# Layer A's out-projection as seven products for eight, in a two-layer f32 trunk

## The chip, the cores and the metric

The kernel runs on one core of one Trainium2 chip. The metric is the device time of one execution in microseconds; of several runs the median counts.

## The reference

Two layers x <- x + mixer(RMSNorm(x)), then a last RMSNorm; x is 2048 x 1024, f32. Both layers end in an out-projection of a 2048 x 1536 tensor z onto 1024 columns:

```python
# layer A
u = h @ w_in                      # 1024 -> 3072: gate, xb
xb = causal_depthwise_conv(xb, conv_w, conv_b)
y = rg_lru(xb, gate_w, gate_b, lam)
x = x + (y * silu(gate)) @ w_out  # z = y * silu(gate)
# layer B
u = h @ w_in                      # 1024 -> 6144: bg, cg, xv, gate
y = bg * causal_depthwise_conv(cg * xv, conv_w)
x = x + (y * silu(gate)) @ w_out
```

## The kernel before, in words

Everything lies transposed: channels on the 128 partitions (P), tokens in four chunks of CH = 512 columns, two chunks to a half. WIDTH = 1536 is twelve blocks of 128 (NH = 12, six pairs KH), 1024 output channels are eight row blocks (KB).

An f32 product is made from f16 parts. Each operand is scaled and split into a high part (ACT, L1119) and a low part (DVE, L1120); `mm3` (L497) issues three matmuls of 128x128 by 128x512, high by high (L500), high by low (L503), low by high (L504). The scale of z comes from its squares: `z_square` (L764) sums the squares of each block on ACT (L769), `scale_from` (L776) sums these over the partitions by a small matmul pt (L780) and works out the scale on DVE (L783 to L789, L1113).

Layer A's in-projection (`in_A`, from about L808) goes through six pairs of heads, for each first the convolution and gates, then SiLU gate and z (L863); the recurrence is a scan on DVE (L906), ahead of it a product on POOL (L905) that uses ACT's square root (L902). Each z is stored to DRAM by `store_z` (L757). Its out-projection is the class `OutProj` (L1126): chunk by chunk, row block by row block, plain block products, 4 x 8 x 12 x 3 matmuls. For chunk 0 the first ten blocks (EARLY) go ahead with a scale of their own (zse), so that their loads and splits run while the in-projection still goes on.

Layer B's two projections use seven products for eight (the form of Strassen and Winograd): a product of 2x2 blocks becomes seven products of sums of blocks. `SEVEN` gives for each name the operand (B11, B21, B22 are blocks of z, T1 to T4 differences), and which output it goes to; A11, A12, A22 and S1 to S4 are blocks and sums of the weights. For layer B's out-projection, `OutSums` (L1304) runs the names in `ORDERS` over each half of the tokens, four row blocks each. `fetch` is its list of loads in order of due time in steps of one row block (a z load at 9 - 2k/3 steps ahead of its product), `splits` that of its splits (6 - 2k/3 ahead). The sums of weights were made in B's in-projection (`weights`) and stored.

Each engine works through its instructions in one order, which the program's scheduler fixes; loads follow one another on SP's queue as `in_order` (L1079) chains them. `defer` and `tick` (L643, L646) put an operation off by some steps, `advance` (L656) gives side work one step beside each group of products. Beside the out-projection `emitA` (L1587) adds the residual, stores x for layer B and adds up its squares on POOL (L230), `besideA` prepares the first operands hB of layer B's in-projection (norms L305, splits L311 and L313).

Of the kernel before, what the change touches and what calls it, by code (L numbers as in the profile page):

```python
# [14 lines left out]
P = 128  # L15
# [31 lines left out]
def trunk(ctx, tc, xT, xn, prm, wa, ga, oa, wb, ob, out):  # L47
# [11 lines left out]
    zd = {  # L59
        (k, c): dr.tile([2 * P, CH], F32, name=f"z{k}_{c}", tag=f"z{k}_{c}")  # L60
        for k in range(NH // 2)
        for c in range(4)
    }

    zt = {
        (half, n, k): dr.tile([P, CH], F32, name=f"z{n}{half}_{k}", tag=f"z{n}{half}_{k}")
# [5 lines left out]
        (n, k): dr.tile([P, 2, CH], F16, name=f"w{n}_{k}", tag=f"w{n}_{k}")  # L72
        for n in ("A11", "A12", "A22", "S1", "S2", "S3", "S4")
# [582 lines left out]
    def advance(side):  # L656

        tick()
        if extra:
            extra[0][0] += 1  # L660
            if extra[0][0] % 3 == 0 and next(extra[0][1], "end") == "end":
                extra.pop()
        while side and next(side[0], "end") == "end":
            side.pop(0)
# [93 lines left out]
    def store_z(kp, m, half, c, z):  # L758
        rows = slice(m * P, (m + 1) * P)
        stores.append(sp.dma_start(zd[kp, 2 * half + c][rows, :], z))  # L760
# [48 lines left out]
    def in_A(ops, first, head, side, before_end, beside):  # L809
# [6 lines left out]
        def pair(hp):  # L816
            heads = (2 * hp, 2 * hp + 1)
            us, tails, sg, gw, taps, gu = {}, {}, {}, {}, [], []

            def conv(m, half, c, a, undo=None):  # L820
# [3 lines left out]
                us[m, half, c] = u = buf(wk, "u", "u", 12)  # L824
# [93 lines left out]
            def xafter(half):  # L918
                side.extend([mixer(half, 0), mixer(half, 1)])
                if half and hp == NH // 2 - 1:  # L920
                    before_end(None)

            def silu(m, half, c, a, undo):
# [7 lines left out]
                sg[m, half, c] = t = buf(wk, "sz", "sg", 8)  # L931
# [8 lines left out]
            def gafter(half):  # L940
                if half == 0 and hp == NH // 2 - 1:
                    before_end(marks[-1])

            units.append((wa[2 * hp], xdest, nothing, beside, xafter, conv))
            units.append((wa[2 * hp + 1], nothing, nothing, beside, gafter, silu))
# [6 lines left out]
    def in_B(ops, first, side, before_end, beside):  # L952
        units = []

        def pair(jp):
# [64 lines left out]
            def gdone(m, half, c, t):  # L1020
# [3 lines left out]
                if late(half):  # L1024
                    g.tensor_tensor(out=t, in0=y, in1=th, op=ALU.mult)
                    z_done(m, half, c, t)
# [3 lines left out]
            def bdone(m, half, c, t):  # L1030
# [3 lines left out]
                else:  # L1034
                    g.tensor_tensor(out=t, in0=t, in1=y, op=ALU.mult)
                    z_done(m, half, c, t)

            zs = {}

            def z_done(m, half, c, z):  # L1040

                zs[m, half, c] = z

                def keep_z(name, t):
                    stores.append(sp.dma_start(zt[half, name, jp], t))

                def diff(name, out, x, y):
                    g.tensor_tensor(out=out, in0=x, in1=y, op=ALU.subtract)
                    keep_z(name, out)

                t1, t2, t4 = cg[0, half, 0], cg[0, half, 1], cg[1, half, 1]
                if (m, c) != (0, 1):
                    keep_z(f"B{m + 1}{c + 1}", z)
                z_square(z, jp, m, half, c, 2 if jp == NH // 2 - 1 or (m, c) == (0, 1) else SQUARED)
                if (m, c) == (0, 1):
                    diff("T1", t1, z, zs[0, half, 0])
                if (m, c) == (1, 1):
                    diff("T2", t2, z, t1)
                if (m, c) == (1, 0):
                    diff("T3", zs[0, half, 1], zs[1, half, 1], zs[0, half, 1])  # L1060
                    diff("T4", t4, z, t2)
# [30 lines left out]
    zse = keep(3)  # L1092

# [3 lines left out]
    LAST = NH // 2 - 1  # L1097
    EARLY = 2 * LAST

# [26 lines left out]
    class OutProj:  # L1126

        def __init__(self, wdram, wsc):  # L1130
            self.wdram, self.wsc = wdram, wsc
            self.rawz, self.raww, self.zops, self.wops = {}, {}, {}, {}
            self.plan, self.done = self.operands(), 0

        def load_z(self, c, kp):
            for m in range(2):
                t = buf(wp, "zr", "zr", 10)
                in_order(sp.dma_start(t, zd[kp, c][m * P : (m + 1) * P, :]))
                self.rawz[2 * kp + m, c] = t

        def load_w(self, k, dh):
            t = buf(wp, "wo", "wo", 8)
            n = (2 * k + dh) * CH
            in_order(sp.dma_start(t, self.wdram[:, n : n + CH]))
            self.raww[k, dh] = t

        def z(self, k, c, zs):
            self.zops[k, c] = split_out(opp, "zs", 22, self.rawz.pop((k, c)), zs[:, 0:1])

        def w(self, k, dh):  # L1150
            if (k, dh) not in self.raww:
                self.load_w(k, dh)
            raw = self.raww.pop((k, dh))
            self.wops[k, dh] = split_out(wp, "wf", 5 * KH, raw, self.wsc[:, 0:1])

        def operands(self):

            for k in range(EARLY):
                self.w(k, 0)
                self.z(k, 0, zse)  # L1160
                yield
            for k in range(EARLY):
                self.w(k, 1)
                yield
            for k in range(EARLY, NH):
                for dh in range(2):
                    self.w(k, dh)
                    yield
            for c in range(4):
                out_scales(zsq[c], zsc[c], self.wsc)  # L1170
                for k in range(0 if c else EARLY, NH):
                    self.z(k, c, zsc[c])
                    yield

        def upto(self, n):
            while self.done < n:
                next(self.plan, None)
                self.done += 1

        def early(self):  # L1180
            out_scales(zsq[0][:, 0:EARLY], zse, self.wsc)

        def start(self, anchor):

            loads.append(anchor)
            for kp in range(LAST):
                self.load_z(0, kp)
                for m in range(2):
                    if kp < 3:
                        self.load_w(2 * kp + m, 0)  # L1190

        def ahead(self):
            for k in range(EARLY):
                self.upto(k + 1)
                yield

        def run(self, emit, end_chunk, side, rest, kept):
            late, xrs = [], {}
            order, fetched = [(c, d) for c in range(4) for d in range(KB)], [0]

            def lag(n):
                while len(late) > n:
                    late.pop(0)()

            def residuals(n):
                while fetched[0] < min(n + XAHEAD, len(order)):
                    c, d = order[fetched[0]]
# [95 lines left out]
    }  # L1303

    class OutSums:

# [551 lines left out]
```

## Time and profile before

| | |
|---|---|
| runs | 1982.82, 1981.59, 1982.82 us; median 1982.82 |
| the profiled execution | 1984.61 us, of which the span from first to last instruction is 1982.7 |
| granted TensorE clock, mean | 0.996 of full speed |
| busy of the span | PE 1959.7 us, DVE 1194.6, ACT 1063.5, POOL 597.6 |
| out-projection of A | its matmuls start at 617.6 and end at 870.4 us; 249.72 us busy |
| data moved | 216.25 MB, mean 109 GB/s |

PE is TensorE, PEld its weight loads, DVE VectorE, ACT ScalarE, POOL GpSimd, SP the engine whose queue starts most transfers. Matmuls overlap: the busy time of a single one is longer than the step from one start to the next. A row of waits names the waiting instruction and the one that released it.

### The profile page before, as it was taken

How to read it: one execution, taken by the hardware profiler on the slowest of the kernel's cores; microseconds unless marked ns; L12 is line 12 of the kernel's file. 1: busy time of each engine (PE TensorE's matmuls, PEld its weight loads, DVE VectorE, ACT ScalarE, POOL GpSimd, SP SyncE). 2: the span in 40 equal slices, each digit the busy share in tenths (PEclk: the TensorE clock that was granted, in tenths of full speed). 3: DMA queues.
4: the chain of work that ended last, by engine and by line, in shares of the span. 5: the costliest groups of instructions: out<-in, count | busy, mean ns of one | idle time of the engine just before them, and what ended most of it. 6: DMA issues, size and time to landing. Idle time of an engine off the chain costs nothing.

```text
span 1982.7 us, 25189 instructions
## 1 busy us (share of the span) xinstructions
PE 1959.7 (99%) x9064; PEld 915.8 (46%) x9064; DVE 1194.6 (60%) x2041; ACT 1063.5 (54%) x1912; POOL 597.6 (30%) x486
## 2 busy tenths in 40 slices
PE   8999999999999999999999999999999999999998
PEld 4444444444444444444444444444444444444446
DVE  7977665667675755379535656746626336454565
ACT  7878786868585533155644443544453452454442
POOL 0001000101000311143553673664553443522221
PEclk9999999999999999999999999999999999999999
DMA  8111212151304734421241241242130030397462
GB/s 299 64 54 59 91 54 88 46 171 44 110 11 138 232 108 160 92 95 43 86 144 43 80 165 43 91 149 70 64 112 32 22 107 22 132 381 258 119 200 86
DMA packets 130958, 216.25 MB, mean 109 GB/s; under 512 B 13200, under 2 KB 41488, under 8 KB 130832
## 3 DMA queue, kind: packets, MB, share of 16 engines
q1 hardware_dynamic: 130384, 213.58, 32.8%
q8 instruction: 71, 1.16, 0.3%
q0 software_dynamic: 448, 1.06, 0.2%
q14 instruction: 55, 0.45, 0.1%
HBM read 152.19 MB, written 62.40 MB: 108 GB/s over the span
## 4 chain that ended last, share of the span: by engine, by line
PE 90%; DVE 6%; ACT 2%; DMA 1%; issue 1%; POOL 0%; SPq 0%; DVEq 0%; ACTq 0%
PE acc L504 15%; PE acc L503 15%; PE acc L500 15%; PE p L504 8%; PE p L500 8%; PE p L503 8%; PE r L500 4%; PE r L504 4%; PE r L503 4%; PE pg L880 3%; PE q L504 2%; PE q L500 2%; PE q L503 2%; DVE op L313 1%; DVE u L843 1%
## 5 line engine op out<-in xcount | busy, mean ns | idle before, releaser
L500 PEld LDWEIGHTS <-wc 128*128 128x128 f16 x2096 | 207.9, 99 | 255.0 <-issue 18.2
L504 PEld LDWEIGHTS <-wc 128*128 128x128 f16 x2096 | 205.2, 98 | 257.4 <-issue 14.2
L503 PEld LDWEIGHTS <-wc 128*128 128x128 f16 x2096 | 205.1, 98 | 257.2 <-issue 22.6
L500 PE MATMUL p<-op,wc 128*128 128x512 f16 x768 | 290.7, 379 | 2.3 <-ACT wc L420 1.2
L503 PE MATMUL p<-op,wc 128*128 128x512 f16 x768 | 291.1, 379 | 0.0
L504 PE MATMUL p<-op,wc 128*128 128x512 f16 x768 | 290.6, 379 | 0.4 <-DVE wc L421 0.4
L503 PE MATMUL acc<-op,wc 128*128 128x512 f16 x752 | 285.4, 380 | 2.8 <-DVE op L313 2.8
L504 PE MATMUL acc<-op,wc 128*128 128x512 f16 x752 | 285.7, 380 | 0.0
L500 PE MATMUL acc<-op,wc 128*128 128x512 f16 x752 | 283.3, 380 | 1.3 <-ACT op L311 1.3
L905 POOL TENSOR_TENSOR u<-fixed,u 128x512 f32<-128x512 f32 x48 | 51.3, 1090 | 557.8 <-ACT fixed L902 557.8
L421 DVE SCALAR_TENSOR_TENSOR wc<-ws,fixed,wc 128x512 f16<-128x512 f32 x104 | 103.4, 999 | 84.7 <-ACT wc L420 74.6
L421 DVE SCALAR_TENSOR_TENSOR wc<-wr,fixed,wc 128x512 f16<-128x512 f32 x122 | 106.9, 894 | 78.0 <-ACT wc L420 66.1
L500 PE MATMUL acc<-zs,wf 128*128 128x512 f16 x384 | 145.5, 379 | 0.0
L503 PE MATMUL acc<-zs,wf 128*128 128x512 f16 x384 | 145.5, 379 | 0.0
L504 PE MATMUL r<-op,wc 128*128 128x512 f16 x384 | 145.5, 379 | 0.0
L503 PE MATMUL r<-op,wc 128*128 128x512 f16 x384 | 145.5, 379 | 0.0
L500 PE MATMUL r<-op,wc 128*128 128x512 f16 x384 | 145.5, 379 | 0.0
L504 PE MATMUL acc<-zs,wf 128*128 128x512 f16 x384 | 145.2, 379 | 0.0
L504 PE MATMUL acc<-op,wf 128*128 128x512 f16 (+1 forms) x384 | 135.3, 352 | 0.0
L503 PE MATMUL acc<-op,wf 128*128 128x512 f16 (+1 forms) x384 | 135.3, 352 | 0.0
L500 PE MATMUL acc<-op,wf 128*128 128x512 f16 (+1 forms) x384 | 135.3, 352 | 0.0
L230 POOL TENSOR_TENSOR sa<-sa,sq 128x512 f32<-128x512 f32 x48 | 67.1, 1398 | 224.9 <-ACT sq L229 177.7
(200 smaller groups left out, 3410.6 us busy)
## 6 DMA issues: line engine op xcount, KB each, us to landing
wr<-in_wb SPq DMA_DIRECT2D x104, 256.0 KB, 3.5
xs<-in_xT SPq DMA_DIRECT2D x48, 256.0 KB, 6.0
z<-sg SPq DMA_DIRECT2D x48, 256.0 KB, 2.0
zr<-z SPq DMA_DIRECT2D x48, 256.0 KB, 5.2
zr<-zT SPq DMA_DIRECT2D x48, 256.0 KB, 5.4
wr<-in_wa SPq DMA_DIRECT2D x44, 256.0 KB, 4.1
zB<-ed SPq DMA_DIRECT2D x36, 256.0 KB, 2.0
zT<-cg SPq DMA_DIRECT2D x36, 256.0 KB, 2.0
```

The source lines that it names most:

```text
L230: squared[0] = eng.tensor_tensor(out=acc, in0=acc, in1=sq, op=ALU.add)
L313: return hi, v.tensor_tensor(out=t[:, 1, :], in0=src, in1=t[:, 0, :], op=ALU.subtract)
L421: v.scalar_tensor_tensor(out=t[:, 1, :], in0=src, scalar=sw[:, 2:3], in1=t[:, 0, :], op0=ALU.mult, op1=ALU.subtract,)
L500: ins = nc.tensor.matmul(acc, wh, xh, start=start, stop=False, **kw)
L503: nc.tensor.matmul(acc, wh, xl, start=False, stop=False, **kw)
L504: return nc.tensor.matmul(acc, wl, xh, start=False, stop=stop, **kw)
L843: v.scalar_tensor_tensor(out=u[:, n:], in0=a[:, 0 : CH - n], scalar=ac(3 - n), in1=u[:, n:], op0=ALU.mult, op1=ALU.add,)
L880: ins = nc.tensor.matmul(pg, gw[m][:, oo], u, start=True, stop=True)
L905: g.tensor_tensor(out=u, in0=w, in1=u, op=ALU.mult)
```

## The change

- `OutProj` goes; layer A's out-projection is an `OutSums("A", ...)`: half 0 in the order S1, S4, A12, A11, S2, S3, A22, half 1 in A11, S2, S3, A22, A12, S1, S4; 2 x 7 x 4 x 6 x 3 matmuls. (Layer B's is the same class; the halved last chunks are for B alone.)
- z's differences T1 to T4 are made on POOL in A's in-projection and stored with the blocks (`z_done`, now shared by both layers).
- The sums S1 and S4 of the weights are made and split in A's in-projection, and stored (12 pairs); the other five names (STAY) are made beside half 0 from raw weights (`load_raw`, `make_w`), and stay for half 1.
- One scale for half 0 from all its squares, in place of the early scale from ten blocks. Buffers: u 12 to 14, sg 8 to 10, wo 8 to 10, zs 22 to 18, new wv of 12.
- x after layer A stays in SBUF for hB (`xh`); the norm of chunk 1 goes over DRAM, that of chunks 0 and 2 over PE (before: chunks 0 and 2 over DRAM, chunk 1 over PE). hB is prepared in the second half.

```diff
+    def z_done(l, kp, m, half, c, z, zs, tiles, steps):
+        zs[m, c] = z
+        def keep_z(name, t):
+            stores.append(sp.dma_start(zt[l, half, name, kp], t))
+        def diff(name, out, x, y):
+            g.tensor_tensor(out=out, in0=x, in1=y, op=ALU.subtract)
+            keep_z(name, out)
+        t1, t2, t3, t4 = tiles
+        if (m, c) != (0, 1):
+            keep_z(f"B{m + 1}{c + 1}", z)
+        z_square(z, kp, m, half, c, steps)
+        if (m, c) == (0, 1):
+            diff("T1", t1, z, zs[0, 0])
+        if (m, c) == (1, 1):
+            diff("T2", t2, z, t1)
+        if len(zs) == 4:
+            diff("T3", t3 or zs[0, 1], zs[1, 1], zs[0, 1])
+            diff("T4", t4, zs[1, 0], t2)
...
-                    store_z(hp, m, half, c, z)
-                    z_square(z, hp, m, half, c)
+                    z_done(
+                        "A", hp, m, half, c, z, zs[half],
+                        [us[i, half, j] for i, j in ((0, 0), (1, 0), (0, 1), (1, 1))],
+                        1 if last else SQUARED,
+                    )
+                    if last and half == 0 and len(zs[0]) == 4:
+                        before_end(stores[-1])
...
-    class OutProj:
...
     class OutSums:
...
+        RAW = {"A11": (0,), "A12": (1,), "A22": (3,), "S3": (0, 2), "S2": (2, 3, 0)}
...
                     for k in range(KH):
                         at = n - 6 + 2 * k / 3
-                        splits.append((at, half, name, k))
+                        splits.append((at, self.split_z, half, name, k))
                         fetch.append((at - 3, self.load_z, half, name, k))
-                        if half == 0 or name not in self.STAY:
+                        if half and name in self.STAY:
+                            continue
+                        if l == "B" or name not in self.STAY:
                             fetch.append((n - 5 + k / 100, self.load_w, half, name, k))
+                            continue
+                        splits.append((at + 0.1, self.make_w, name, k))
+                        for r in self.RAW[name]:
+                            fetch.append((at - 2.9, self.load_raw, name, k, r))
...
                 for name, a in combinations(raw):
...
+                    if (self.l, name, k) in wt:
+                        sp.dma_start(wt[self.l, name, k], self.split_w(wk, "wy", 2, a))
+                        yield
+                    if self.l == "A" and name == "S4":
+                        break
...
+        def make_w(self, name, k):
+            raw = [self.raw.pop((name, k, n)) for n in self.RAW[name]]
+            a = raw[0]
+            for n, b in enumerate(raw[1:]):
+                t = buf(wp, "ws", "ws", 2)
+                add = name == "S2" and n == 0
+                g.tensor_tensor(out=t, in0=a, in1=b, op=ALU.add if add else ALU.subtract)
+                a = t
+            self.wops[name, k] = self.split_w(wp, "wf", 5 * KH, a)
...
-            if half:
+            if half and self.l == "B":
                 steps[5:] = [(name, ts) for ts in (FIRST, SECOND) for name in order[5:]]
...
-        inv_of(sums[c], inv[c // 2][c % 2], g if c in (0, 2) else None)
+        steps = inv_between(sums[c], inv[c // 2][c % 2], g if c == 1 else None)
```

Three places show how the order of the instructions moves (line numbers of the change differ from those of before). ACT's queue around the first splits for the out-projection; zs is a split z, sg a gate and later z, tg, pg, a and fixed belong to the gates, and fixed<-sg (L786, in the kernel before L769) is a sum of squares. Before, inside the last pair of heads:

```order
L902 ACTIVATE fixed_226<-fixed_226 128x1024
L884 ACT_TABLE_LOAD
L884 ACTIVATE tg0_4767<-pg_4765,fixed_226 128x512
L1119 ACTIVATE zs_4993<-zr_4932,fixed_226 128x512
L1119 ACTIVATE zs_5001<-zr_4934,fixed_226 128x512
```

and with the change, at the end of half 0's gates:

```order
L786 ACTIVATE fixed_298<-sg_5180 128x512
L786 ACTIVATE fixed_298<-sg_5186 128x512
L926 ACT_TABLE_LOAD
L926 ACTIVATE fixed_298<-fixed_298 128x1024
L955 ACT_TABLE_LOAD
L955 ACTIVATE sg_5332<-acc_5270,fixed_298 128x512
L1115 ACTIVATE zs_5305<-zr_5197,fixed_298 128x512
L1115 ACTIVATE zs_5344<-zr_5199,fixed_298 128x512
L955 ACTIVATE sg_5337<-acc_5271,fixed_298 128x512
L1115 ACTIVATE zs_5347<-zr_5201,fixed_298 128x512
L1115 ACTIVATE zs_5376<-zr_5203,fixed_298 128x512
```

The splits have moved from ahead of the last pair's gates to behind the last squares of half 0, and stand among gate instructions of half 1.

POOL's queue at the end of the in-projection; u is the recurrence's input, and in the change (L764) also the tile that a difference is written to; ws are sums of weights, sa of squares. Before:

```order
L905 TENSOR_TENSOR u_4605<-fixed_226,u_4605 128x512
L905 TENSOR_TENSOR u_4705<-fixed_226,u_4705 128x512
L905 TENSOR_TENSOR u_4714<-fixed_226,u_4714 128x512
L484 TENSOR_TENSOR ws_5745<-wr_5703,wr_5704 128x512
L484 TENSOR_TENSOR ws_5809<-ws_5745,wr_5701 128x512
L484 TENSOR_TENSOR ws_5945<-wr_5702,ws_5809 128x512
L230 TENSOR_TENSOR sa_5565<-sa_5565,sq_5612 128x512
```

and with the change:

```order
L764 TENSOR_TENSOR u_4695<-sg_5180,sg_5083 128x512
L764 TENSOR_TENSOR u_4702<-sg_5186,u_4695 128x512
L764 TENSOR_TENSOR u_4766<-sg_5186,sg_5180 128x512
L764 TENSOR_TENSOR u_4775<-sg_5088,u_4702 128x512
L929 TENSOR_TENSOR u_4979<-fixed_298,u_4979 128x512
L929 TENSOR_TENSOR u_4988<-fixed_298,u_4988 128x512
L764 TENSOR_TENSOR u_4870<-sg_5409,sg_5332 128x512
L764 TENSOR_TENSOR u_4879<-sg_5415,u_4870 128x512
L764 TENSOR_TENSOR u_4979<-sg_5415,sg_5409 128x512
L764 TENSOR_TENSOR u_4988<-sg_5337,u_4879 128x512
L1233 TENSOR_TENSOR ws_5890<-wo_5753,wo_5755 128x512
L1233 TENSOR_TENSOR ws_5892<-ws_5890,wo_5757 128x512
```

Differences of z stand in the queue ahead of the recurrence's last products (half 0) and behind them (half 1); the sums for S2 begin right behind the last of them, where sums for layer B's first unit stood.

SP's queue at the start of the out-projection's loads; zr is a z read back, wo a raw weight block, wv a stored sum. Before, in the last pair of the in-projection:

```order
L1138 DMA zr_4932<-z0_0_76 128x512
L760 DMA z3_1_89<-sg_3449 128x512
L1138 DMA zr_4934<-z0_0_76 128x512
L1144 DMA wo_4936<-in_oa 128x512
L1144 DMA wo_4938<-in_oa 128x512
L1138 DMA zr_4940<-z1_0_80 128x512
L1138 DMA zr_4942<-z1_0_80 128x512
```

and with the change:

```order
L761 DMA zAT40_5_117<-u_4775 128x512
L1213 DMA zr_5197<-zAT10_0_94 128x512
L1213 DMA zr_5199<-zAT10_1_95 128x512
L1213 DMA zr_5201<-zAT10_2_96 128x512
L1213 DMA zr_5203<-zAT10_3_97 128x512
L1213 DMA zr_5205<-zAT10_4_98 128x512
L1213 DMA zr_5207<-zAT10_5_99 128x512
L1221 DMA wv_5209<-wAS1_0_244 128x2x512
L1213 DMA zr_5211<-zAB220_0_88 128x512
L1221 DMA wv_5213<-wAS1_1_245 128x2x512
```

The first z loads have moved behind the store of T4 of half 0's last pair; the six weights S1 come among the z of S1 and of S4.

## Rows read from the trace of the kernel before

**Rows 1.** The page: span; busy us (share of the span) x instructions of each engine.
```profile
span 1982.7 us, 25189 instructions
...
PE 1959.7 (99%) x9064; PEld 915.8 (46%) x9064; DVE 1194.6 (60%) x2041; ACT 1063.5 (54%) x1912; POOL 597.6 (30%) x486
```

**Rows 2.** Waits of PE, whole run: waited for, us in total, times, longest us.
```profile
PE acc L503 <- DVE op L313: 2.8, 3, 1.7
...
PE p L500 <- ACT wc L420: 1.2, 1, 1.2
...
PE p L500 <- DVE pb L543: 0.8, 1, 0.8
...
PE p L504 <- DVE wc L421: 0.4, 1, 0.4
```

**Rows 3.** Windows: length, busy us of PE, PEld, DVE, ACT, POOL (x), PEclk, DMA share, GB/s.
```profile
200.00:300.00 100.00, 100.00 (x432) 45.34 (x433) 65.82 (x131) 79.15 (x136) 10.36 (x10) 1.00 0.22 72
587.00:618.00 31.00, 31.00 (x140) 14.33 (x139) 20.51 (x41) 24.44 (x40) 4.28 (x4) 1.00 0.16 58
650.00:700.00 50.00, 49.90 (x239) 23.36 (x238) 35.59 (x61) 30.28 (x56) 17.18 (x12) 1.00 0.82 273
700.00:800.00 100.00, 100.00 (x474) 46.56 (x473) 50.56 (x82) 31.10 (x51) 16.79 (x13) 1.00 0.32 114
```

**Rows 4.** Groups by form, PE: operands, tile, count | busy us, mean ns | idle before.
```profile
L503 PE MATMUL acc<-zs,wf 128*128 128x512 f16 x384 | 145.5, 379 | 0.0
...
L262 PE MATMUL pn<-dg,fixed 128*128 128x128 f32 x48 | 6.5, 280 | 0.0
```

**Rows 5.** Timeline of PE, 834 to 850 us: start us, us, instruction.
```profile
833.67 0.38 PE L500 MATMUL acc<-zs,wf 128*128 128x512 f16 x1
...
849.86 0.38 PE L500 MATMUL acc<-zs,wf 128*128 128x512 f16 x1
```

**Rows 6.** Timeline of all engines around the end of half 0's squares.
```profile
603.39 0.62 ACT L769 ACTIVATE fixed<-sg 128x512 f32<-128x512 f32 x1
...
604.54 0.29 PE L780 MATMUL pt<-fixed 128*128 128x12 f32 x2
...
606.34 0.16 DVE L783 TENSOR_REDUCE fixed<-pt 128x1 f32<-128x12 f32 x1
...
607.77 2.14 POOL L905 TENSOR_TENSOR u<-fixed,u 128x512 f32<-128x512 f32 x2 [11.41 <-ACT fixed L902]
...
608.90 2.09 DVE L906 TENSOR_TENSOR_SCAN u<-a,fixed,u 128x512 f32<-128x512 f32 x1 [2.03 <-POOL u L905]
...
611.34 0.21 DVE L1113 TENSOR_SCALAR fixed<-fixed 128x1 f32<-128x1 f32 x1
```

**Rows 7.** Groups by form of ACT, DVE and POOL.
```profile
L230 POOL TENSOR_TENSOR sa<-sa,sq 128x512 f32<-128x512 f32 x48 | 67.1, 1398 | 224.9 <-ACT sq L229 177.7 <-DMA xo<-x 46.6
...
L484 POOL TENSOR_TENSOR ws<-wr,ws 128x512 f32<-128x512 f32 x26 | 41.0, 1578 | 11.3 <-ACT pre L799 5.8 <-POOL ws L484 2.0 <-DMA wS<-wy 1.5
...
L1120 DVE SCALAR_TENSOR_TENSOR zs<-zr,fixed,zs 128x512 f16<-128x512 f32 x48 | 39.3, 848 | 11.1 <-ACT zs L1119 11.0
...
L1048 POOL TENSOR_TENSOR cg<-ed,cg 128x512 f32<-128x512 f32 x24 | 32.0, 1334 | 1.8
...
L1119 ACT ACTIVATE zs<-zr,fixed 128x512 f16<-128x512 f32 x48 | 31.8, 710 | 6.9 <-POOL sa L230 2.9 <-DVE zs L1120 1.6 <-DVE fixed L1113 0.8
```

**Rows 8.** Timeline of SP's queue, layer B's out-projection, first half.
```profile
1741.53 0.33 SPq L1375 DMA_DIRECT2D xo<-x  x1
1742.21 0.32 SPq L1362 DMA_DIRECT2D zr<-zB  x1
```

**Rows 9.** Windows in the same stretch.
```profile
1725.00:1735.00 10.00, 10.00 (x49) 4.70 (x48) 3.79 (x12) 1.75 (x4) 4.74 (x3) 1.00 1.02 356
1765.00:1775.00 10.00, 10.00 (x48) 4.53 (x47) 5.47 (x8) 2.56 (x4) 0.00 (x0) 1.00 1.07 389
```

**Rows 10.** Timeline of DVE, 712 to 720 us.
```profile
713.29 4.73 DVE L305 SCALAR_TENSOR_TENSOR xs<-xs,fixed,inv 128x512 f32<-128x512 f32 x7 [11.56 <-DMA inv<-rd]
```

More of the change, by code (lines that the diff above doesn't have):

```diff
@@ L71, in trunk @@
     wt = {
[L72 to L73 removed]
+        (l, n, k): dr.tile([P, 2, CH], F16, name=f"w{l}{n}_{k}", tag=f"w{l}{n}_{k}")
+        for l, names in (("A", ("S1", "S4")), ("B", ("A11", "A12", "A22", "S1", "S2", "S3", "S4")))
+        for n in names
         for k in range(NH // 2)
@@ L658, in advance @@
         tick()
[L659 to L662, printed above, removed]
+        for e in list(extra):
+            e[0] += 1
+            if e[0] % e[1] == 0 and next(e[2], "end") == "end":
+                extra.remove(e)
         while side and next(side[0], "end") == "end":
@@ L1382, in split, with split_z @@
         def split(self):
-            _, half, name, k = self.splits.pop(0)
+            _, make, *what = self.splits.pop(0)
+            make(*what)
+        def split_z(self, half, name, k):
             raw = self.raw.pop((half, name, k))
-            self.zops[half, name, k] = split_out(opp, "op", NOP, raw, zsc[half][:, 0:1])
+            pool, tag, bufs = (opp, "op", NOP) if self.l == "B" else (opp, "zs", NZS)
+            self.zops[half, name, k] = split_out(pool, tag, bufs, raw, zsc[half][:, 0:1])
         def scales(self, half):
@@ L1551, in trunk, with follows @@
     preA, preB = out_scale(oa, wsc[0]), out_scale(ob, wsc[1])
-    def follows(l, wdram, t, side):
-        o = (OutProj if l == "A" else OutSums)(wdram, t)
+    def follows(l, wdram, t):
+        o = OutSums(l, wdram, t)
         def start(anchor):
-            if anchor is None:
-                o.early()
-            else:
-                o.start(anchor)
-                side.append(o.ahead())
-        return o, start
-    def beside_units(pre, once, twice):
-        n = [0]
-        def beside(half):
-            n[0] += 1
-            for _ in range((n[0] > once) + (n[0] > twice)):
-                next(pre, None)
-        return beside
@@ new lines, in start, with rest_of_extra, emitA @@
+            extra.append([0, 1, o.ahead()])
+        return o, start
+    def rest_of_extra():
+        while extra:
+            run(extra.pop(0)[2])
+    outA, startA = follows("A", oa, wsc[0])
+    extra.append([-24, 3, outA.weights(preA)])
+    in_A(hA, w0, head, sideA, startA, nothing)
+    while sideA:
+        advance(sideA)
+    rest_of_extra()
+    hB, inv, sums, w0 = [{}, {}], {}, {}, {}
+    early, sws = [], []
+    xh, ended = [{}, {}], {}
+    def emitA(c, d, x, ts, ins):
+        sp.dma_start(x2[c][d * P : (d + 1) * P, :], x)
+        xh[c // 2][d, c % 2] = x
+        n = ended[c] = ended.get(c, 0) + 1
+        if n == 1:
@@ L1645, in trunk @@
+        if n == 35:
+            for ks in ((0, 1), (2, 3)):
+                early.append(build_h(1, xh[0], inv[0], ks, hB[0], (0,)))
+            early.append(unit_weights(1, wb[0], w0, sws[0]))
+        if n >= 52:
+            for kk in range(2 * n - 104, 2 * n - 102):
+                normed(1, xh[1][kk, 0], kk, inv[1][0])
+        while early and next(early[0], "end") == "end":
+            early.pop(0)
+    outA.run(emitA, endA, besideA)
+    x = xh[1]
     while early:
```

317 lines of the change are left out of this document (61 added, 256 removed).

## The prediction

> **What bounds the kernel now.** I read the page first: TensorE (PE) is busy for 1959.7 of 1982.7 us, no other engine for more than 60% [rows 1]. The waits of PE next: none is in layer A's out-projection; three on low parts of layer B's operands sum to 2.8 us, and the start of layer B's in-projection holds 1.2 + 0.8 + 0.4 = 2.4 us [rows 2]. The windows then show the stage that is changed: PE is busy for 31.00 of 31 us before the out-projection of layer A begins and for all of 700 to 800 us within it, while DVE has half of that time free and ACT more [rows 3]. So the stage is bounded by the number of matmuls and by nothing else, and a matmul less is time less, as long as what the new form wants from DMA, POOL and DVE arrives in time. That is the question of the whole prediction.
>
> **The matmuls.** Before, 3 x 384 = 1152 matmuls acc<-zs,wf of 128x512 [rows 4]. Seven products for eight: 2 halves x 7 names x 4 row blocks x 6 blocks x 3 = 1008, so 144 fewer. A row's duration (379 ns) overlaps the next one's, so the price is the step from start to start: in 834 to 850 us the first start is at 833.67 and the 75th after it at 849.86, all of this kind, 16.19 / 75 = 0.2159 us [rows 5]. 144 x 0.2159 = **31.1 us**. Small ones: the column sums of squares go from five pairs to two larger ones (0.29 us a pair [rows 6]), -0.9 us; the inverse norms of one more chunk go over PE, a group of eight pn matmuls, 6.5 / 6 = 1.1 us [rows 4], +1.1 us (for two chunks it took the way over DRAM, now for one). Sum on PE: **-30.9 us**. The granted clock in these stretches is 1.00, the 2.4 GHz level [rows 3]; PE is as full after as before, so I let it stay.
>
> A rule that speaks against this sum: the Trainium skill, "TensorE: Matmul & The Clock Gate", section "Back-to-back issue gap", gives about 131 ns for each matmul of 512 columns in a stream with weight loads, which would make it 144 x 0.131 = 18.9 us, an estimate from that page, and a time near 1965. The trace disagrees: it is such a stream, a weight load per matmul, and its step is 0.2159 us over 75 matmuls.
>
> **The boundary from in-projection to out-projection.** Before, chunk 0's first ten heads got a scale of their own, and eight splits ran on ACT long before the first product at about 617.6 us. Now one scale is made from all 24 squares of half 0, then come splits. The chain in the trace: the last of these squares on ACT at 603.39, the column sum on PE at 604.54, its reduction on DVE at 606.34, then DVE sits in a scan from 608.90 and the scale is out at 611.34 + 0.21 [rows 6]. The changed order puts four z differences on POOL ahead of the product that this scan waits for (order of POOL below the change): the last z is there at about 602.8, so the last two or three differences end near 606.6 (1.33 us each [rows 7]), and that product had to wait for ACT until 607.77 anyway, so they cost nothing. Its cover is thin: with 1 us more each the scan is late by 1 us. I put the scale at 612.3. S1 wants six splits; ACT does one in 0.71, DVE its low part in 0.85 [rows 7], with gate work between (order of ACT): the sixth is ready near 619.5; the first row block uses it after 15 matmuls, 617.6 + 15 x 0.2159 = 620.8. The weights S1 stand in SP's queue behind T4's store (about 606.7): 13 loads at 0.68 us, 615.5, and some 4.5 us to land, 620. Both fit by about 1 us. Wait **0 to 3 us; I take 1**, since two margins are near nothing.
>
> **Half 0's supply.** Here the five kept weights are made from raw blocks: 48 loads instead of 24, 18 sums on POOL. The narrowest place is S2, three raw blocks and two sums for each k. In SP's order its last raw load is the 105th from the first z load (S1, S4, A12, A11 with z, residuals and layer B's raw weights ahead of it). The nearest rows are those of layer B's own first half, which loads in the same manner: one load's issue to the next takes 1742.21 - 1741.53 = 0.68 us [rows 8], and the windows there show 389 and 356 GB/s [rows 9], that is 262,144 bytes / 389 = 0.67 us and / 356 = 0.74 us. From 607: 105 x 0.68 = 71.4, landing some 5.3, two sums of 1.5 (1.58 at most [rows 7]), a split of 1.5: ready at 688. S2 starts after four names of 72 matmuls, 617.6 + 288 x 0.2159 = 679.8; in it all four row blocks go through k together, so the last k is wanted 60 matmuls later, 692.7. Slack 4 us, less what POOL loses: 12 sums x 1.5 and four additions of squares x 1.4 are 24 us against 15.5 us in which PE uses S2, begun some 14 us ahead. I count **2 us of slack and no wait at 0.68; 2 to 4 us of wait at 0.74** (105 x 0.06 = 6 us later).
>
> **Half 1.** Weights stay, so loads are few. DVE: up to the last split of z there are about 128 operations of 512 columns (40 low parts, some 25 residual additions, then layer B's norms and operands). By 0.676 us (seven in 4.73 us [rows 10]) that is 86.5, by the dearest, 0.848 [rows 7], 108.5 us; half 1 lasts 504 x 0.2159 = 108.8 us and its splits begin some 23 us earlier. Covered by both prices; **0**, and if POOL slowed DVE to 1.1 us each, 9 us.
>
> **In-projection A.** Each pair of heads (about 100 us) gets eight z differences on POOL and, for S1 and S4, three sums, 8 x 1.3 + 3 x 1.5 = 15 us on an engine with 10.36 of 100 us busy; DVE and ACT get two more weight splits, 2.6 and 1.4 us, on 65.82 and 79.15 [rows 3]. The z stores grow from 48 to 84, behind none that PE waits for but the last. POOL beside DVE is what I can't price: from nothing to about 2 us in all. **I take 0.5.** The start of layer B's in-projection keeps its 2.4 us; layer B's own order is unchanged. A gain there is the lower bound: h is built from x kept in SBUF, not read back.
>
> **Sum.** 1 + 0 + 0.5 = 1.5 us of new waits: -30.9 + 1.5 = -29.4. The profiled execution took 1984.61 us (span 1982.7 and 1.9 around it); it becomes 1955.2. It stands 1.8 above the median of 1982.82, so for the median **1953.4 us**. A measurement of this kernel tells 0.2%, about 4 us, from no change.
>
> **Rivals.**
> - *S2 or the boundary comes late.* Loads at 356 GB/s, the lowest window of [rows 9], or POOL's sums at 1.6 us with additions between them: 4 to 8 us more, **1957 to 1962**. For it: 0.68 us leaves 2 us of slack. Against: layer B's same form shows no wait of PE on weights there. The Trainium skill, "DMA: Bandwidth & Descriptors", section "Where 436 GB/s comes from", puts the bound from HBM at about 358 GB/s. The trace agrees for one of the windows and shows 389 in another, so the page would make this case the likely one and the rows make it the lesser.
> - *DVE or POOL binds elsewhere*: half 1 at 1.1 us per operation, or the in-projection with POOL's differences beside DVE's scans: 3 to 8 us, **1956 to 1962**. Against: half of DVE's time is free from 700 us on.
> - *Slower, by the supply of S2.* Weights made beside the half, not stored, hold PE at one place: each 0.01 us per load moves S2's end by 1.05 us. To lose 31 + 4 us beyond 2 to 4 us of slack, a load would have to take 0.68 + 38 / 105 = 1.04 us, 252 GB/s: **above 1987**. The out-projection of A itself now reaches 273 GB/s at a DMA share of 0.82, in a stretch that isn't saturated (650 to 700 us [rows 3]); that rate would give 0.96 us a load and 1953 + 105 x 0.28 - 3 = 1979. For it: SP's queue also holds stores that wait for the in-projection's last z, and a load behind a waiting store waits too.
>
> **How the numbers follow.** Forecast as above (1950 to 1957) 0.62; S2 or the boundary late 0.2; DVE or POOL elsewhere 0.11; supply at 273 GB/s or several of these together, 1962 to 1979, 0.02; slower 0.03, no change 0.02. The range takes the first three: from 1950 (no new wait, 2 us of the 2.4 at layer B's start gone) to 1962. Faster by over 0.2%: 0.62 + 0.2 + 0.11 + 0.02 = 0.95; within 0.02; slower 0.03.
>
> **What would show it.** Right: 720 matmuls acc<-zs,wf and 288 with the stored weights, 0.216 us apart; the out-projection 31 us shorter between the same first and last products; no PE wait over 2 us in it; DMA near 380 GB/s from 610 to 690 us. Late S2: PE waiting on a low part of wf near 680 to 693 us, POOL's sum or a wo load behind it. Late boundary: a wait on zs at the first product, the scan ahead of the scale. Wrong outright: waits in in-projection A that were not there, a granted clock under 1.00 behind one of these waits, or a step of matmuls other than 0.216.

## The result, and the profile after

The changed kernel takes 1993.23 us (median of 5, 1990.43 to 1996.68) against 1982.82 before: ratio 1.0052, interval [1.0038, 1.0067]. It was forecast 29 us faster and is 10 us slower, outside the range; a rival had that sign, but not this mechanism. Lines of the changed kernel's profile have numbers of their own (split_out is L1115 and L1116, make_w's sums L1233 and its splits L1188 and L1189, z's differences L764, the additions of squares L227).

The page of the changed kernel (span, then busy time, share and count of each engine), against [rows 1]:

```profile
span 1992.2 us, 25454 instructions
...
PE 1943.2 (98%) x8922; PEld 905.2 (45%) x8922; DVE 1276.9 (64%) x2094; ACT 1100.8 (55%) x1967; POOL 728.0 (37%) x568
```

PE has 16.5 us less to do, DVE 82 more and POOL 130 more, in a span that is 9.5 us longer. Where that lies is read from the first and last starts of the out-projection's products (operands, count, ns min/median/max, first to last start):

```profile
L497 PE MATMUL acc<-zs,wf x240: 376/379/634, 663.7 to 835.7; 128*128 128x512 f16 x120
...
L497 PE MATMUL acc<-zs,wv x96: 377/379/634, 632.4 to 877.1; 128*128 128x512 f16 x96
```

The first product starts at 632.4, before at 617.6; layer B's first at 877.8, before at 870.6. So **the in-projection of layer A lost 14.8 us, the out-projection gained 7.6 instead of 31, and layer B lost 2.3**: 14.8 - 7.6 + 2.3 = 9.5. The median matmul is still 379 ns; the slowest is 634, which is the 1.2 GHz level of the clock.

The 14.8 us hide a part. Between 10 and 30 us the execution of the kernel before ran for a while at the slow clock, and that of the changed kernel didn't:

```profile
10.00:30.00 20.00, 18.35 (x47) 9.15 (x46) 15.15 (x56) 14.96 (x29) 0.00 (x0) 0.83 1.04 388
```

```profile
10.00:30.00 20.00, 17.49 (x54) 8.72 (x53) 17.14 (x57) 16.30 (x31) 0.00 (x0) 1.00 1.03 383
```

(before, then changed; the columns are those of [rows 3].) So the same matmul of the in-projection, the 241st acc<-op,wc, starts at 101.40 us, before at 103.96: 2.6 us ahead. From there to the first product the changed kernel lost 14.8 + 2.6 = **17.4 us**. This "loss from 100 us on" is the better measure, and is given for the experiments too. The waits of PE (waited for, us in total, times, longest):

```profile
PE ss L233 <- POOL sa L227: 7.4, 3, 6.4
...
PE pn L259 <- DVE dg L256: 4.7, 3, 3.9
PE pg L904 <- ACT tg L908: 3.9, 1, 3.9
PE acc L497 <- DVE u L871: 3.3, 1, 3.3
...
PE acc L497 <- DVE xo L1300: 2.5, 1, 2.5
PE acc L497 <- DVE fixed L866: 2.3, 1, 2.3
...
PE acc L497 <- DVE sg L956: 1.8, 1, 1.8
```

None of these rows is among [rows 2], those of the kernel before. The u (L871), fixed (L866), tg and sg rows lie in the in-projection, at 122, 181, 215 and 339 us: 3.3 + 2.3 + 3.9 + 1.8 = 11.3 us. Behind the first three the granted clock was at half, the 1.2 GHz level:

```profile
126.60:129.90 3.30, 3.30 (x9) 1.22 (x8) 0.05 (x1) 1.60 (x5) 0.00 (x0) 0.50 0.86 273
184.60:188.00 3.40, 3.40 (x7) 1.28 (x6) 1.70 (x4) 2.23 (x3) 1.61 (x2) 0.50 0.41 157
218.80:225.50 6.70, 6.05 (x11) 2.38 (x12) 5.05 (x9) 5.03 (x12) 0.00 (x0) 0.50 0.69 216
```

From 100 us on the steps of the matmuls acc<-op,wc and pg add up to 6.9 us more than before. 11.3 + 6.9 = 18.2, near the 17.4. The other waits lie in the out-projection: 2.5 at 710, 6.4 at 754, 0.4 and 4.7 near 847 to 860, together 14.0; its matmuls at the slow clock cost 6.3 us more than at full clock. The column sums and pn take 7.5 us instead of 4.1, partly at the slow clock. -31.1 + 14.0 + 6.3 + 3.4 = -7.4, near the measured -7.6. Of layer B's 2.3 us, 2.0 are matmuls at the slow clock from 932 to 935 us, behind waits of 1.2 and 0.4 us that the kernel before has too [rows 2], with no fall of the clock behind them: not a cost of the change that any run here shows.

The windows answer to [rows 3]:

```profile
200.00:300.00 100.00, 96.06 (x405) 43.23 (x404) 68.28 (x130) 71.19 (x121) 30.16 (x22) 0.97 0.31 103
650.00:700.00 50.00, 50.00 (x238) 23.09 (x237) 33.72 (x60) 27.19 (x48) 18.81 (x13) 1.00 1.04 389
700.00:800.00 100.00, 91.14 (x410) 42.16 (x409) 79.69 (x105) 49.12 (x81) 32.39 (x22) 0.93 0.75 250
```

In 200 to 300 us POOL has three times as much to do; in 700 to 800 PE lost 8.9 us, DVE went from 50.56 to 79.69 and the granted clock to 0.93. In 650 to 700 us the loads run at 389 GB/s and PE waits for none of them.

**The longest wait** is in two views, POOL's timeline and PE's (start us, us, instruction, idle time before it and what ended it):

```profile
745.74 0.92 POOL L249 DMA_DIRECT2D rd<-r  x1
758.01 0.56 POOL L250 DMA_DIRECT2D inv<-rd  x1 [11.35 <-DMA rd<-r]
758.59 2.61 POOL L227 TENSOR_TENSOR sa<-sa,sq 128x512 f32<-128x512 f32 x2
```

```profile
761.25 1.87 PE L233 MATMUL ss<-fixed,sa 128*128 128x1 f32 x8 [6.39 <-POOL sa L227]
...
763.36 0.63 PE L500 MATMUL acc<-zs,wf 128*128 128x512 f16 x1
```

POOL writes chunk 1's inverse norms to DRAM (rd) and stands 11.35 us until they are there, before it issues the read (inv). Two additions of squares (sa) for chunk 0 are in its queue behind that, and PE's column sums (ss) behind these. Then the clock is down for twelve matmuls.

**The wait at 710 us** is DVE's, and its rows show why beside POOL's:

```profile
698.10 0.74 DVE L1300 SCALAR_TENSOR_TENSOR xo<-acc,fixed,xo 128x512 f32<-128x512 f32 x1
...
701.01 3.43 DVE L1116 SCALAR_TENSOR_TENSOR zs<-zr,fixed,zs 128x512 f16<-128x512 f32 x2
...
707.71 0.74 DVE L1116 SCALAR_TENSOR_TENSOR zs<-zr,fixed,zs 128x512 f16<-128x512 f32 x1
708.38 1.75 DVE L1189 SCALAR_TENSOR_TENSOR wf<-ws,fixed,wf 128x512 f16<-128x512 f32 x1
...
712.39 2.06 DVE L1300 SCALAR_TENSOR_TENSOR xo<-acc,fixed,xo 128x512 f32<-128x512 f32 x3
```

```profile
697.58 1.72 POOL L1233 TENSOR_TENSOR ws<-ws,wo 128x512 f32<-128x512 f32 x1
...
707.87 3.38 POOL L1233 TENSOR_TENSOR ws<-wo 128x512 f32<-128x512 f32 x2 [0.63 <-DVE wf L1189]
```

```profile
713.18 0.38 PE L497 MATMUL acc<-zs,wf 128*128 128x512 f16 x1 [2.47 <-DVE xo L1300]
```

A low part of z or of a weight (two operands in SBUF) takes 0.74 us at 707.71, where POOL pauses, and 1.7 to 1.75 us beside POOL's sums; the residual addition xo<-acc,fixed,xo, one operand of which is in PSUM, takes 0.74 at 698.10 in the middle of a sum. Of all such rows between 632 and 878 us that lie wholly beside POOL or wholly clear of it, zs takes 1.36 against 0.74 us on average (10 and 47), xo<-acc 0.74 against 0.74 (14 and 36). The Trainium skill says this, "SBUF — State Buffer", section "Who interferes with whom": an instruction of VectorE with two inputs in SBUF contends with one of GpSimd that reads SBUF, and one with at most one such input, outside the modes that use two ports, doesn't. The trace agrees on both counts.

The same in the in-projection, at 120 to 126 us: DVE, POOL, PE:

```profile
120.74 0.84 DVE L871 SCALAR_TENSOR_TENSOR u<-fixed,u 128x1 f32<-128x1 f32 x1
...
122.17 0.64 DVE L871 SCALAR_TENSOR_TENSOR u<-fixed,u 128x1 f32<-128x1 f32 x1
...
124.61 0.20 DVE L871 SCALAR_TENSOR_TENSOR u<-fixed,u 128x2 f32<-128x2 f32 x1
```

```profile
120.30 1.27 POOL L764 TENSOR_TENSOR u<-sg,u 128x512 f32<-128x512 f32 x1 [3.92 <-DVE sg L882]
121.53 1.26 POOL L764 TENSOR_TENSOR u<-sg 128x512 f32<-128x512 f32 x1
122.75 1.26 POOL L764 TENSOR_TENSOR u<-sg,u 128x512 f32<-128x512 f32 x1
```

```profile
125.75 0.38 PE L497 MATMUL acc<-op,wc 128*128 128x512 f16 x1 [3.33 <-DVE u L871]
...
127.08 0.63 PE L501 MATMUL acc<-op,wc 128*128 128x512 f16 x1
...
130.03 0.38 PE L497 MATMUL acc<-op,wc 128*128 128x512 f16 x1
```

Corrections of the convolution's first columns (L871, one to three columns) take 0.84 and 0.64 us beside z's differences and 0.20 after them. PE waits 3.33 us for the PSUM tile that this chain frees, then is slow until 130 us.

### The profile page after: what moved, and what is told of

It reads as the page before. It is cut to its first block, busy times and chain, and to the rows that moved or that the text cites. A ratio compares the mean times of both kernels' runs of the same rounds, so it can differ in the third digit from the quotient of the medians.

```text
span 1992.2 us, 25454 instructions
## 1 busy us (share of the span) xinstructions
PE 1943.2 (98%) x8922; PEld 905.2 (45%) x8922; DVE 1276.9 (64%) x2094; ACT 1100.8 (55%) x1967; POOL 728.0 (37%) x568
## 4 chain that ended last, share of the span: by engine, by line
PE 80%; issue 7%; DVE 6%; ACT 3%; DMA 2%; POOL 1%; DVEq 0%; POOLq 0%; ACTq 0%; SPq 0%
PE acc L497 12%; PE acc L501 12%; PE acc L500 12%; PE p L501 8%; PE p L497 8%; PE p L500 8%; PE r L497 4%; PE r L500 4%; PE r L501 4%; PE pg L904 2%; PE q L500 2%; PE q L501 2%; PE q L497 2%; DVE u L930 1%; DVE op L310 1%
## 5 line engine op out<-in xcount | busy, mean ns | idle before, releaser
L227 POOL TENSOR_TENSOR sa<-sa,sq 128x512 f32<-128x512 f32 x48 | 74.6, 1554 | 202.9 <-ACT sq L226 199.9
L1300 DVE SCALAR_TENSOR_TENSOR xo<-acc,fixed,xo 128x512 f32<-128x512 f32 (+1 forms) x120 | 84.6, 709 | 99.0 <-PE acc L501 98.6
L993 POOL TENSOR_TENSOR pb<-pb,cg 128x512 f32<-128x512 f32 x48 | 68.8, 1433 | 187.5 <-DVE fixed L391 99.2
L862 DVE SCALAR_TENSOR_TENSOR u<-acc,fixed,u 128x511 f32<-128x511 f32 (+2 forms) x138 | 100.9, 742 | 51.5 <-ACT u L860 51.5
L417 ACT ACTIVATE wc<-wr,fixed 128x512 f16<-128x512 f32 x122 | 83.6, 711 | 78.7 <-DVE fixed L394 77.1
L904 PE MATMUL pg<-u,gts 128*128 128x512 f32 x192 | 98.7, 607 | 3.9 <-ACT tg L908 3.9
L481 POOL TENSOR_TENSOR ws<-wr 128x512 f32<-128x512 f32 x52 | 78.1, 1503 | 59.1 <-DVE wc L418 29.3
```

The costliest lines, as they stand in the source:

```text
L227: squared[0] = eng.tensor_tensor(out=acc, in0=acc, in1=sq, op=ALU.add)
L417: last_hi[0] = s.activation(t[:, 0, :], src, AF.Copy, scale=sw[:, 2:3])
L481: g.tensor_tensor(out=t, in0=x, in1=y, op=op)
L862: v.scalar_tensor_tensor(out=u[:, n:], in0=a[:, 0 : CH - n], scalar=ac(3 - n), in1=u[:, n:], op0=ALU.mult, op1=ALU.add,)
L904: ins = nc.tensor.matmul(pg, gw[m][:, oo], u, start=True, stop=True)
L993: g.tensor_tensor(out=t, in0=t, in1=cg[m, half, c], op=ALU.mult)
```

## The experiments

Each is an edit of the changed kernel unless it says so. "First product" is the start of the out-projection's first matmul, 632.4 us in the changed kernel and 617.6 before. The table has it from the traces, with the loss from 100 us on against the kernel before, and how much of that lies between the 601st and the 701st matmul acc<-op,wc (206 to 238 us in the changed kernel), where PE waits for the gate's tg:

| run | first product, us | loss from 100 us on | of that at 206 to 238 us |
|---|---|---|---|
| changed kernel | 632.4 | 17.4 | 8.1 |
| e1, no differences | 628.7 | 12.7 | 9.1 |
| e2, differences on DVE | 622.6 | 8.2 | 0.9 |
| e8, before with differences | 621.8 | 3.9 | 0.0 |
| e9, side work later | 630.9 | 13.5 | 7.9 |
| e11, e9 and no differences | 626.4 | 11.1 | 9.3 |
| e10, all moved | 617.3 | 3.4 | 0.9 |

Each row is one execution; the measured times are medians.

**e1: no differences.** `diff` stores x for layer A, with no subtraction.

```diff
+            if l == "A":
+                keep_z(name, x)
+                return
             g.tensor_tensor(out=out, in0=x, in1=y, op=ALU.subtract)
```

> Leaves out the subtractions of T1 to T4 in layer A's in-projection: one operand is stored in their place; stores, loads and buffers stay. Theory (POOL's differences lengthen DVE's operations beside them, DVE frees PE's buffers late): the three waits of PE on DVE at 122, 181 and 339 us (3.3, 2.3, 1.8) and the slow clock behind the first go, the first out-projection product comes at 623 to 625 instead of 632.4, the time is 1983 to 1987. The wait on ACT at 215 us (3.9) has another cause and stays. Rival (the 36 more stores and the tiles they hold are what delays): product at 632, time 1993.

Measured 1982.78 us (ratio 1.0003 [0.9994, 1.0012]); first product at 628.7. The waits on DVE fell to 1.0, 1.4 and 1.2 us, that on ACT stayed (4.1). The first product is 3.7 us earlier, half of what was expected; the loss from 100 us on is 4.7 us less, 5.6 outside the last column of the table. So the contention is real, and about 5 us of the in-projection's loss. The time fell by more, 10.4 us in the median. In the traces it is 8.9: 2.2 more lie in the out-projection, and 3.0 in layer B, whose slow stretch at 932 us this execution doesn't have.

**e2: differences on DVE.**

```diff
-            g.tensor_tensor(out=out, in0=x, in1=y, op=ALU.subtract)
+            (v if l == "A" else g).tensor_tensor(out=out, in0=x, in1=y, op=ALU.subtract)
```

> All of the computation stays; layer A's z differences run on DVE instead of POOL. Theory (contention of POOL with DVE): DVE gets 48 x 0.66 = 32 us more and loses about 17 us of lengthening in 550 us, but nothing is lengthened at the places where PE waits; waits in the in-projection fall from 11 to 4 to 8 us, time 1986 to 1991. Rival (DVE's work in all is what counts): waits grow to 15 us, time 1996 or more.

Measured 1982.87 us (1.0001 [0.9989, 1.0012]), 3 us below the range expected and the same as with no differences (e1). First product at 622.6; the profiled execution was a fast one (1978.37). The wait of 4 us on ACT has gone. PE's and ACT's instructions there stand in the same order as in e1, and ACT runs its four splits of weights ahead of the gate in both. What differs is where the gate's product goes. PE and ACT in the changed kernel, then in e2:

```profile
219.45 2.07 PE L904 MATMUL pg<-u,gts 128*128 128x512 f32 x2 [3.94 <-ACT tg L908]
218.71 0.69 ACT L908 ACTIVATE tg<-pg,fixed 128x512 f32<-128x512 f32 x1
```

```profile
213.58 1.02 PE L904 MATMUL pg<-u,gts 128*128 128x512 f32 x2
215.19 0.69 ACT L908 ACTIVATE tg<-pg,fixed 128x512 f32<-128x512 f32 x1
```

In the changed kernel, in e1, e9 and e11 the program puts this product into PSUM bank 5, where the product two before it lies (207.58 us in the changed kernel), and ACT reads that one only at 218.71, behind a square root and four splits. In e2 it goes to bank 7 and in e10 to bank 6, where no earlier product is still to be read, and PE doesn't wait. So 7 of the 9 us by which e2's loss is smaller (17.4 to 8.2) come with the other bank, and not from what DVE and POOL take for the work. Why the program chose bank 5 is open.

**e3: chunk 1's inverse over PE.**

```diff
-        steps = inv_between(sums[c], inv[c // 2][c % 2], g if c == 1 else None)
+        steps = inv_between(sums[c], inv[c // 2][c % 2], None)
```

> Chunk 1's inverse norms over PE, not over DRAM on POOL's queue. Theory (POOL stands 11.35 us behind its own transfer, two additions of chunk 0's squares behind it, PE's column sums behind these): PE's wait of 6.4 us at 754 us and 2.6 us of slow clock go, eight pn matmuls come (1.1 us): 8 us less, 1984 to 1987. Rival (POOL is late because of the sums for S2 and S3): a wait on sa of 4 us or more stays, 1989 to 1993.

Measured 1985.29 us (1.0015 [1.0006, 1.0025]). The out-projection takes 237.0 us from its first product to its last, 8.1 less. The row of PE's waits:

```profile
PE ss L233 <- POOL sa L227: 1.8, 3, 0.9
```

From 6.4 to 0.9 us at its longest: it was POOL's own transfer that made it long.

**e4: no sums of weights beside half 0.** `make_w` splits the first raw block.

```diff
-            for n, b in enumerate(raw[1:]):
+            for n, b in enumerate(()):
```

> Leaves out the 18 sums of layer A's weights for S2 and S3 beside half 0 (their first raw block is split instead); loads stay. Theory: the wait of 2.5 us on DVE at 710 us and 1.7 us of slow clock go, the wait of 6.4 us on POOL stays since it is the transfer's: 1988 to 1990. Rival (the sums make POOL late): both go, 1980 to 1983. If POOL's sums cost nothing: 1993.

Measured 1982.20 us (1.0004 [0.9994, 1.0013]). The out-projection is 7.5 us shorter (237.6); the wait at 710 is gone, that on POOL is 3.3 instead of 6.4. (The profiled execution, 1986.81 us, was the slowest of this run.) So both theories have a part: the transfer makes this wait, and the sums, by which POOL came to it later, lengthened it.

**e5: e2 and e3 together.**

> Layer A's z differences on DVE and chunk 1's inverse over PE, both at once. Theory (two separate losses, 10.4 and 7.9 us, that add): 1993.2 - 18.3 = 1975, 1972 to 1978. Rival (a wait that goes lets the next one show): 1979 to 1985.

Measured 1974.34 us (0.9955 [0.9940, 0.9969]): the two losses add, as the theory had it.

**e6: e5, and the 18 sums of `make_w` on DVE** (v for g in its `tensor_tensor`).

> As the one with both, and the 18 sums of layer A's weights on DVE too. Theory (POOL's sums hold up DVE's operations with two operands in SBUF, and delay POOL's additions of squares): the wait on the residual addition at 710 us and on the squares at 739 go, DVE gets 12 us and is rid of 8 to 12 us; 3 to 5 us less than the one with both: 1970 to 1973. Rival (DVE is full in 700 to 740 us whoever adds): same as the one with both or 2 us more.

Measured 1972.66 us (0.9952 [0.9935, 0.9969]). The median is 1.7 us under e5's, less than the runs' spread; in the trace the wait on the residual addition (1.9 us in e5) is gone and the out-projection 2.2 us shorter, while the wait on POOL's squares is 1.5 us instead of 0.9.

**e7: e6 with `for n in (2, 4) if c == 2 else (2, 3)`.**

> As the one before, and the column products pn of chunk 2's inverse norms one step (some 3.9 us) later on PE. Theory (PE stands 3 to 4 us before pn since the reciprocal root comes late behind DVE's queue, and runs at the slow clock after it): 4 us less, 1965 to 1970. Rival (the norms that wait for pn come late in turn and layer B's in-projection starts late): no change.

Measured 1972.94 us (0.9949 [0.9931, 0.9967]). pn kept its place in PE's order, so nothing was tested; it repeats e6.

**e8: the kernel before, with 48 differences on POOL** behind its `z_square`, into the tiles us of the same pair.

```diff
+                    t = us[m, half, c]
+                    zz = zs[half]
+                    if (m, c) == (0, 1):
+                        g.tensor_tensor(out=t, in0=z, in1=zz[0, 0], op=ALU.subtract)
...
```

> The kernel before with 48 differences of z added on POOL in layer A's in-projection, written over tiles no longer needed and not stored. Theory (POOL beside DVE alone makes the in-projection's waits): two or three waits of PE of 1.5 to 4 us with slow clock behind them, 5 to 10 us more than before, 1987 to 1992. Rival (the waits come from the stores, the weights' sums or the new order): 1982 to 1984.

Measured 1986.42 us (1.0020 [1.0010, 1.0029]), 3.8 more than before and just under the range expected; first product at 621.8, 4.1 us later. Two waits that the kernel before doesn't have (L848 is a copy of the convolution's last columns, L891 a gate's product):

```profile
PE acc L500 <- DVE fixed L848: 1.7, 1, 1.7
...
PE pg L891 <- DVE sg L945: 1.2, 1, 1.2
```

The price of POOL's differences, alone, is 4 us, near the 5 of e1.

**e9: the side work later.** In the changed kernel the squares of the out-projection's weights run on ACT from 48 to 168 us, in the kernel before from 125 to 415.

```diff
-    extra.append([-24, 3, outA.weights(preA)])
+    def held(n, steps):
+        for _ in range(n):
+            yield
+        yield from steps
+    extra.append([-24, 3, held(14, outA.weights(preA))])
```

> The changed kernel with one edit: the side work on layer A's out-projection weights (24 squares for their scale, then S1 and S4) starts 42 steps later in the in-projection, at some 130 us instead of 40. Theory (ACT and DVE have no time left between 50 and 220 us, and the change put these squares there): the waits at 122, 181 and 215 us (9.5 us) and the slow clock behind them (3.2 us) fall to 5 us or less in all, the first out-projection product comes at 622 to 627 instead of 632.4, the time is 1983 to 1988. Rival (POOL's differences are all of it): 1991 to 1994.

Measured 1989.21 us (1.0037 [1.0025, 1.0049]), first product at 630.9. Between the two: 4.0 us in the median; in the trace 1.5 at the first product, but 3.9 from 100 us on. The wait at 122 fell from 3.3 to 1.6, the one at 339 went, those at 181 and 215 stayed.

**e11: e9 without the subtractions.**

> The changed kernel with the side work 42 steps later, and the subtractions of layer A's T1 to T4 left out (one operand is stored in their place). Theory (early side work and POOL's differences together are the in-projection's loss): waits of 2 us or less in all before the out-projection, whose first product comes at 616 to 621; out-projection as in the changed kernel, so 1978 to 1982. Rival (stores or buffers): first product after 624.

Measured 1982.74 us (1.0002 [0.9992, 1.0012]), first product at 626.4. A miss: the waits on DVE are down to 1.4 us and less, but 4.1 us on ACT's gate and the slow clock behind it remain, as in e1: 9.3 of the 11.1 us of the table. That is the PSUM bank (e2), which neither the differences nor the side work makes.

**e10: e6 and e9 together.**

> The one with differences and weight sums on DVE and the inverse over PE, and the side work 42 steps later as well. Theory: its five waits between 136 and 200 us (5.9 us) shrink to 1 to 3 us: 1968 to 1970. Rival (DVE's 32 us of differences alone make these waits): 1972 to 1974.

Measured **1965.71 us** (1964.85 to 1966.90; 0.9914 [0.9898, 0.9931]), 16.4 us under the kernel before in the same comparison (1982.06) and 27.5 under the changed one. That is below the 1968 to 1970 expected. First product at 617.3; from 100 us on 3.4 us of the in-projection's 17.4 are left. The out-projection takes 232.9 us from first product to last, 12.2 less than in the changed kernel. What is left of the waits on DVE and POOL:

```profile
PE pn L259 <- DVE dg L256: 4.1, 3, 3.2
...
PE acc L497 <- DVE fixed L866: 2.3, 2, 1.5
PE ss L233 <- POOL sa L227: 1.9, 2, 1.5
...
PE acc L497 <- DVE sg L956: 1.1, 2, 0.7
```

**e12: e10, with pn later.** `(2, 5)` for chunk 2, and the norms in three steps from step 53 on.

> The one with everything moved (1965.7), and chunk 2's column products pn two steps later, with the norms that use them one step later (three, three and two in the last steps instead of two in each of four). In the order of PE pn now stands 34 matmuls (7 us) later. Theory (PE stands 3.2 us before pn because the root comes late, and runs slow for 1.3 us after it): both go, 4 to 5 us less, 1960 to 1962. Rival (the norms become late and layer B's in-projection waits at its start instead): 1964 to 1967.

Measured 1966.48 us (0.9925 [0.9911, 0.9938]): the rival. In the trace pn stands 17 matmuls later, not 34. The wait before it is down to 0.7 us, and one of 5.1 us stands at the start of layer B's in-projection, where DVE has no idle time:

```profile
PE p L497 <- ACT wc L417: 5.1, 1, 5.1
...
PE pn L259 <- DVE dg L256: 1.4, 2, 0.7
```

```profile
880.00:900.00 20.00, 17.40 (x80) 7.58 (x78) 20.00 (x32) 8.46 (x15) 10.59 (x8) 1.00 0.12 40
```

PE's order was only half of that wait. The split wc that PE waits for is ACT's, and ACT stands 8.95 us for a scale that DVE works out behind its other work (L394). That DVE has more to do up to layer B's start than it has time isn't shown: from 845 to 905 us it is busy for 54.07 of 60. What is shown is that it is full where PE first needs it.

## Why the prediction was wrong, step by step

- **The matmuls: right.** 1008 of them, 0.216 us apart at full clock, so 31.1 us less work. Most of it was given back as waits.
- **The boundary: right.** The first product waits for nothing. Its six splits are ready at about 631.5 us and the sixth is used at 632.4 + 3.2 = 635.7: a margin of 4 us where 1 was forecast.
- **Half 0's supply: the loads right, the sums wrong.** Loads ran at 389 GB/s, the upper of the two rows in [rows 9], S2's blocks came in time, and the slower rival by loads above 1.04 us was not what happened. The step counted POOL's sums as 24 us of POOL and left out what they do to DVE and to POOL's later work: without them the out-projection is 7.5 us shorter (e4), of which 3.1 are the shorter wait behind POOL's transfer. With that transfer gone, moving them to DVE (e6) gives 2.2 us in the trace, and in the median less than the runs' spread. The bound of about 358 GB/s that the prediction cited from the Trainium skill ("DMA: Bandwidth & Descriptors", section "Where 436 GB/s comes from") is passed in this stretch: the trace disagrees, with 389.
- **The inverse norms: the step that failed most in the out-projection.** "For two chunks it took the way over DRAM, now for one" priced PE's products and not POOL's queue. Behind the transfer stood two additions, behind them PE. 8.1 us (e3). The trace of the kernel before has the wait, 35.4 us in all at its four such transfers, and the order of POOL what would stand behind it; the prediction used neither:

```profile
POOL inv L253 <- DMA rd<-r: 35.4, 4, 10.2
```

- **In-projection A: 0.5 us taken, 14.8 measured at the first product and 17.4 from 100 us on.** The prediction's bound, "from nothing to about 2 us", came from POOL's and ACT's busy shares over 100 us, and its second rival put POOL beside DVE at 3 to 8 us for the whole kernel, with a chance of 0.11: the mechanism was seen, its size wasn't. Shares don't tell it. Before the change DVE had a quarter of its time free where the first two waits then came:

```profile
100.00:150.00 50.00, 50.00 (x220) 22.86 (x218) 37.66 (x81) 37.31 (x64) 4.28 (x4) 1.00 0.19 59
150.00:200.00 50.00, 49.58 (x204) 22.54 (x203) 37.31 (x78) 44.18 (x71) 6.42 (x6) 1.00 0.17 53
```

  PE waits on single chains, not on shares. The differences make 4 to 5 us of the loss (e1, e8), the early side work 4 (e9). Some 8 us, the wait on ACT at 215 us and the slow clock behind it, are a PSUM bank that the program gave out otherwise (e2): they go when the differences run on DVE and stay when they are left out (e1, e11). No step of the prediction asked which bank a product would get. With the differences on DVE and the side work later, 3.4 us are left (e10). One reading was wrong as well: the three waits on L313, 2.8 us, are not on layer B's operands but on layer A's, at 51 to 55 us; they enter no sum.
- **Half 1: 0 taken, 4.7 us of wait and its slow clock measured.** The sum of 128 operations went up to the last split of z. It should have gone to layer B's start, with what PE needs there (pn, the norms, first weights): e12 shows that the wait moves there when it goes here.
- **The clock: "I let it stay".** In the changed kernel each of the six waits of PE of 2.3 us or more between 100 us and layer B's start had a stretch at the 1.2 GHz level in it or behind it, with matmuls 0.43 us apart instead of 0.216: 6.9 us in the in-projection and 6.3 in the out-projection, with 2.0 in layer B about 15 us. The wait of 3.3 us cost 5. The granted clock in 760 to 780 us was 0.79. A wait didn't always bring it: none followed the 1.8 us at 339, nor 2.65 us near 136 in e2. The prediction had named this, a clock under 1.00 behind a new wait, as a sign of being wrong outright.

With the causes taken away (e10) the kernel gains 16 of the forecast 29 us; the waits listed at e10 are 9 of the other 13.

## What to carry to other kernels

When work goes to POOL, price what it does to DVE: each of its operations that reads SBUF lengthens the DVE operation with two SBUF operands beside it by 0.6 to 1 us here. With the differences on DVE the kernel took no longer than with none (e2, e1), but most of what e2 won in the in-projection was a PSUM bank, so that DVE being the cheaper place isn't shown apart from that. Before giving POOL a transfer that waits, read its queue behind it, down to the PE instruction at the end of that chain. When a new wait on a PSUM tile appears, look at which product had its bank before and who still has to read it. A matmul saved is a gain only where the engines that feed it have time left in that very stretch: look at windows of 20 us for each engine, up to the next point where PE needs them, and add to each expected wait the slow clock behind it.

## What the runs showed of the hardware that was not expected

- DVE slows by operand, not by kind: a correction of one column (L871) took 0.77 us on average where it lay wholly beside POOL (4 rows) and 0.21 clear of it (31); a 512-column operation with an operand in PSUM took 0.74 both ways.
- The clock can fall behind a wait or in it. At 125.75 us the first matmuls after 3.33 us of wait still took 379 ns, those from 126.65 to 129.21 634 ns, and those from 130.03 on 379 again. In the wait of 6.39 us that ended at 761.25 the granted clock was 1.00 up to 758 and 0.50 from there:

```profile
754.90:758.00 3.10, 0.00 (x0) 0.00 (x0) 0.00 (x0) 0.00 (x0) 0.00 (x0) 1.00 0.58 9
758.10:761.20 3.10, 0.00 (x0) 0.00 (x0) 0.00 (x0) 0.00 (x0) 3.00 (x3) 0.50 0.56 120
```

- POOL stood 11.35 us until a write of 2 KB to DRAM from its own queue was known as done, in a stretch (745.7 to 758 us) in which the DMA engines were busy for 0.33 of the time and moved 27 GB/s: want of bandwidth wasn't the reason, and the rows show no other. In the kernel before the four such writes took 8.7 to 10.4 us to land.
